# Experts 12 and 13 combined one at a time, the last expert's rows gathered during expert 14, and experts 13 and 14 added to them by padded products

## The chip, the cores and the metric

The kernel runs on one core of one Trainium2 chip. The metric is the device time in microseconds (us), the median of several runs. TensorE (PE in the views, with PEld for its weight loads), VectorE (DVE), ScalarE (ACT), GpSimd (POOL) and SyncE (SP) each work through a queue of their own in order, and wait for one another by semaphores. SP's queue issues the DMA transfers of the weights.

## The reference

One layer on 512 tokens of 1024 numbers: three attention branches, a gated sum, a norm, and then a mixture of 16 experts, in which every expert chooses its 64 best tokens, followed by a second norm. The change lies in the experts and the second norm alone:

```python
    gate, idx = lax.top_k(jnp.swapaxes(aff, 1, 2), cap)      # cap = 64 tokens for each of 16 experts
    xs = x[bidx, idx]
    h = jnp.einsum('becd,edf->becf', xs, w_gate_up)
    hg, hu = jnp.split(h, 2, axis=-1)
    ye = jnp.einsum('becf,efd->becd', jax.nn.silu(hg) * hu, w_down)
    ye = ye * gate[..., None].astype(ye.dtype)
    return jnp.zeros_like(x).at[bidx, idx].add(ye)
...
        x = layer_norm(DN_ALPHA * x + ffn, ln2_g[l], ln2_b[l])
```

## The kernel before

**An expert.** Expert e has 12 MB of float32 weights, which come from memory in blocks of 2 MB, and of 1 MB at the end. `gate_up(e, (k,))` multiplies the 64 chosen rows by slice k of the first weights (k = 0 to 7, eight matmul instructions for each k, shown as `g` x4 and `u` x4, line 1328). `act_h` makes the hidden rows on ACT and DVE, `h_transpose` turns them on PE (`ht`, line 1370, with a copy to `hT` on ACT), and `down(e)` multiplies them by the second weights (`y`, 32 instructions, line 1384). `down` then splits its result into a high and a low part by `hi_lo`, once for each half of the columns: a cast on ACT (line 103), then a subtraction on DVE (line 104).

**The order of the work** is written out by hand in the loop over e, and each engine keeps it. For the middle experts: `gate_up` for k below `lead(e)` (4, and 2 for expert 14, 1 for expert 15), just ahead of the last of these the function `full_mode(e)`, then `down(e - 1)`, then `gate_up` for the other k. So expert e - 1 is finished inside expert e.

**The combine.** The 64 result rows of an expert are added to their tokens' rows in `acc` (4 blocks m of 128 tokens, each of two halves o of 512 columns) by a product with a 0/1 matrix. `slots_T(pr)` makes that matrix on PE (`gT`, line 1407) and ACT copies it to SBUF as `GT` or `GTe`. Experts are combined in pairs: `combine(pr, half)` adds pair pr to two blocks m, with two products (high and low part) into a PSUM bank `cb` for each m and o (8 products in all, line 1468), and a DVE addition to `acc` behind each bank (line 1476). Banks of the tag `mm` are three, used in turn. Pair 5 (experts 10 and 11) is combined in the `full_mode` of experts 13 and 14, pair 6 (12 and 13) in expert 14 behind k = 3 and k = 5, and expert 14 alone in expert 15 by `combine_last`, whose products use two banks `ab`, with the norm's sums taken on the way.

**The last expert's rows** take a shorter way: the 64 rows of expert 15 are gathered from `acc` into the bank `zb` by `last_rows` (line 1551: blocks 0 and 1 at the start of expert 15, blocks 2 and 3 at its end, when expert 14 is already in these). Since blocks 0 and 1 are gathered before expert 14 is added, `last_own` adds expert 14's share to them by two products with `same` (a matrix of slots that hold the same token, made by `same_rows` and padded with zeros to write both halves). `last_down` then adds the products of the second weights straight onto `zb` (line 1577), and norms these rows and scatters them over the output. The other tokens are normed and written to the output by `norm_mean` to `norm_bias` while expert 15 runs (ACT lines 1528 and 1542, POOL line 1545).

**SP's queue** issues the weight blocks in order. Each issue waits until its place in SBUF is free, and until the block eight places earlier has landed.

Of the kernel before, what the change touches and what calls it, by code (L numbers as in the profile page):

```python
# [9 lines left out]
F32 = mybir.dt.float32  # L10
# [34 lines left out]
def pair_of(e):  # L45
    return divmod(e, 2)

# [28 lines left out]
def layer_kernel(ctx: ExitStack, tc: tile.TileContext, xt, xn, first0, wu, bgate, rpb, gains, wrt,  # L76
# [935 lines left out]
    run(g_na_proj())  # L1012
    top = cp.tile([48, 64], F32, name="top")

# [361 lines left out]
    def down(e):  # L1376
        hT = HT.pop(e)
        y = PB("Y", f"y{e}")
        for k in range(4):
            w = ring.get("dn", e, k)  # L1380
            for j in range(2):
                hf, c = divmod(2 * k + j, 4)
                for o in range(2):
                    nc.tensor.matmul(y[o * 64:o * 64 + 64], hT[:, c, hf * 64:hf * 64 + 64],  # L1384
                                     w[j][:, o * 512:(o + 1) * 512],
                                     start=(k == 0 and j == 0), stop=(k == 3 and j == 1))
            ring.done("dn", e, k)
        pr, ep = pair_of(e)
        if ep == 0:
            both = R("VS" if pr % 2 else "raw", [P, 2, D], f"y{pr}", F32R)  # L1390
            YP[pr] = (both[:, 0], both[:, 1])
        yh, yl = YP[pr]
        r = slice(ep * 64, ep * 64 + 64)
        for o in range(2):
            c = slice(o * 512, (o + 1) * 512)
            if pr == 7:
                hi_lo(yh[:64, c], yh[64:, c], y[o * 64:o * 64 + 64])
            else:
                hi_lo(yh[r, c], yl[r, c], y[o * 64:o * 64 + 64])

    GT = {}

    def slots_T(pr):
        qd, h = divmod(pr, 2)
        gp = PB("mm", f"gT{pr}", (P, NT, P))
        for m in range(NT):
            nc.tensor.matmul(gp[:, m], OH[qd][:, m, h * P:(h + 1) * P], id16, start=True, stop=True)
        if pr < 2:
            homes.append(R("tmp", [P, NT, P], "GT", F32R, bufs=2) if pr else R("bf", [P, NT, P], "GTe", F32R))
        GT[pr] = g = homes[1 + pr % 2]  # L1410
        if pr < 7:
            nc.scalar.copy(g, gp)
        else:
            for i in (0, 64):
                nc.scalar.copy(g[i:i + 64], gp[:64])

# [54 lines left out]
    def combine(pr, half):  # L1471
        for m in (2 * half, 2 * half + 1):
            for o in range(2):
                cb = PB("mm", f"cb{pr}{m}{o}")
                a = add_part(cb, pr, m, o, YP[pr])
                nc.vector.tensor_tensor(a, a, cb, op=ALU.add)  # L1476

    def combine_last(m, sums, banks):
        for o in range(2):
            a = add_part(banks[o], 7, m, o, YP[7][:1])  # L1480
            nc.vector.scalar_tensor_tensor(a, banks[o], 1.0, a, op0=ALU.mult, op1=ALU.add, accum_out=sums[:, m, o:o + 1])
# [65 lines left out]

    def last_rows(zb, ms):
        for m in ms:
            for o in range(2):  # L1550
                nc.tensor.matmul(zb[o * 64:o * 64 + 64], LATE["oh"][:, m], acc_of(m)[:, o * 512:o * 512 + 512],
                                 start=(m == 0), stop=False)

    def same_rows(sm):
        oh = OH[3]
        for m in range(2):
            nc.tensor.matmul(sm[:, :CAP], oh[:, m, 2 * CAP:], oh[:, m, last], start=(m == 0), stop=(m == 1))
        t = R(ring.free_at_end.pop(0), [P, 3, CAP], "same", F32R)
        nc.gpsimd.memset(t[:, 0:3:2].bitcast(F32), 0.0)
        for i in (0, 64):  # L1560
            nc.scalar.copy(t[i:i + 64, 1], sm[:64, :CAP])
        t = t.rearrange("p a s -> p (a s)")
        LATE["same"] = [t[:, CAP:], t[:, :2 * CAP]]

    def last_own(zb):
        y = YP[7][0]
        for o in range(2):
            nc.tensor.matmul(zb, LATE["same"][o], y[:, o * 512:o * 512 + 512], start=False, stop=False)

# [30 lines left out]
    def full_mode(e):  # L1600
# [7 lines left out]
        elif e == 4:  # L1608
            residual_rows(0)
        elif e == 5:  # L1610
            combine(0, 1)
        elif e > 5:
            combine((e - 3) // 2, (e + 1) % 2)
        if e % 2 and e > 3 or e == NEXP - 2:
            slots_T(e // 2)
        if e < 3 or e == NEXP - 2:
            h_transpose(e - 1)

    for e in range(NEXP):
        if e == 0:  # L1620
# [3 lines left out]
            all_of(g0)  # L1624
        elif e < NEXP - 1:
            for k in range(lead(e)):
                if k == lead(e) - 1:
# [17 lines left out]
            for k in range(lead(e), KD):  # L1645
                if e == 2 and k == lead(e):
                    steps(nrm)
                gate_up(e, (k,))
                if e == 1 and k == 5:
# [5 lines left out]
                elif e == 12 and k == 5:  # L1655
                    late_row(0)
                    late_row(1)
                elif e == 13 and k == 5:
                    late_half(2, "gh")
                    late_half(3, "bh")  # L1660
                    slot_tables()
                elif e == NEXP - 2 and k in (3, 5):
                    combine(6, k // 5)
        else:
            gate_up(e, (0,))
            zb, *ab = (PB("mm", f"end{i}") for i in range(3))
            last_rows(zb, (0, 1))
            h_transpose(e - 1, ab[0])
            down(e - 1)
            for m in range(NT):  # L1670
                gate_up(e, (1 + m,))
                if m == 0:
                    same_rows(ab[1])
                    LATE["g"] = [ln_row(2, h, f"g2{h}", "ST"[h]) for h in range(2)]
# [15 lines left out]
            last_own(zb)  # L1690
            last_rows(zb, (2, 3))
            last_down(zb, last_transpose(h, (ab[0], PB("Y", "htl"))))
# [131 lines left out]
```

## Time and profile before

| what | us |
|---|---|
| median of 3 runs | 949.57 (948.92 to 949.93) |
| the profiled execution, its own time | 948.83 |
| its span | 947.1 |
| PE busy | 923.2 (97%) |
| DVE, ACT, POOL busy | 432.7, 281.9, 104.2 |

The span is the profiler's stretch from the first to the last instruction, and the time holds 1.7 us around it. All points in time below are us from the span's start. A PE row's duration ends at a modelled end that lies after the next row's start, so what a piece of PE work costs is read as the distance between the starts of two rows.

### The profile page before, as it was taken

The page shows a single profiled execution, that of the slowest core. Times are in us where ns is not written, and L with a number is a line of the kernel's source. Part 1 is how long each engine was busy: PE and PEld are TensorE (multiplying, and loading weights), DVE is VectorE, ACT ScalarE, POOL GpSimd, SP SyncE. Part 2 cuts the span into 40 slices and gives each one's busy share as a digit, 9 for nine tenths or more (in the row PEclk, how much of TensorE's full clock was granted, in tenths as well). Part 3 has the DMA queues.
Part 4 walks back from the last instruction along what each step waited for, and adds up shares of the span by engine and source line. Part 5 has one row for each costly group of instructions (what it writes and reads, how often), then busy time and mean ns, then how long its engine had stood idle before and what let it go on. Part 6 is the DMA issues. An engine that isn't in the chain of part 4 may idle for free.

```text
span 947.1 us, 12783 instructions
## 1 busy us (share of the span) xinstructions
PE 923.2 (97%) x5200; PEld 599.7 (63%) x5200; DVE 432.7 (46%) x795; ACT 281.9 (30%) x532; POOL 104.2 (11%) x123
## 2 busy tenths in 40 slices
PE   9999999999999999999999999999999998999996
PEld 8899888788888888888886433533353333533334
DVE  6347659775476576237454111562232222322233
ACT  5434443654444454233242111110010100111122
POOL 0102303000122231000023004000000000000005
PEclk9999999999999999999999999999999999999999
DMA  9322221221433322566929999999999999999996
GB/s 362 120 68 67 68 67 45 67 76 37 117 98 100 104 84 69 228 246 255 381 75 381 422 427 421 421 427 427 428 428 428 426 430 425 428 428 428 427 421 260
DMA packets 40282, 251.41 MB, mean 265 GB/s; under 512 B 13136, under 2 KB 13520, under 8 KB 24992
## 3 DMA queue, kind: packets, MB, share of 16 engines
q1 hardware_dynamic: 40144, 250.34, 66.1%
q8 instruction: 41, 0.67, 0.3%
q0 software_dynamic: 80, 0.26, 0.1%
q14 instruction: 17, 0.14, 0.0%
HBM read 247.44 MB, written 2.36 MB: 264 GB/s over the span
## 4 chain that ended last, share of the span: by engine, by line
PE 79%; DMA 12%; DVE 5%; ACT 2%; issue 1%; POOLq 0%; POOL 0%; ACTq 0%; SPq 0%; DVEq 0%
DMA w<-in_wx 12%; PE g L1328 9%; PE u L1328 9%; PE y L1384 8%; PE gate L286 4%; PE gate L288 4%; PE gate L287 4%; PE cb L1468 2%; PE pr L286 2%; PE pr L287 2%; PE pr L288 2%; PE nqk L287 2%; PE nqk L288 2%; PE nqk L286 2%; PE ga L1288 1%; PE pv L662 1%
## 5 line engine op out<-in xcount | busy, mean ns | idle before, releaser
L1328 PE MATMUL g<-w,xs 128*64 128x512 f32 x508 | 132.7, 601 | 9.7 <-DMA w<-in_wx 9.6
L1328 PE MATMUL u<-w,xs 128*64 128x512 f32 x508 | 130.6, 592 | 0.0
L1384 PE MATMUL y<-w,hT 128*64 128x512 f32 x480 | 105.6, 592 | 0.7 <-ACT hT L1374 0.7
L104 DVE TENSOR_TENSOR y<-y,y 64x512 fp32r<-64x512 f32 x30 | 20.7, 689 | 146.2 <-ACT y L103 146.2
L1328 PEld LDWEIGHTS u<-w,xs 128*64 128x64 f32 x508 | 36.5, 137 | 72.5 <-issue 72.2
L1328 PEld LDWEIGHTS g<-w,xs 128*64 128x64 f32 x508 | 32.6, 136 | 72.6 <-issue 52.6
L104 DVE TENSOR_TENSOR los<-raw_twin,whi 128x1024 fp32r<-128x1024 f32 x41 | 53.6, 1307 | 53.5 <-ACT whi L103 53.5
L1384 PEld LDWEIGHTS y<-w,hT 128*64 128x64 f32 x480 | 34.3, 137 | 69.0 <-issue 65.4
L288 PE MATMUL gate<-xh,los 128*128 128x512 f32 x192 | 74.8, 390 | 0.0
L1476 DVE TENSOR_TENSOR acc<-acc,cb 128x512 f32<-128x512 f32 x56 | 34.7, 681 | 56.9 <-PE cb L1468 56.9
L103 ACT CAST y<-y 64x512 fp32r<-64x512 f32 x30 | 17.4, 580 | 139.9 <-PE y L1384 128.7
L286 PE MATMUL gate<-xh,whi 128*128 128x512 f32 x144 | 57.0, 396 | 0.0
L287 PE MATMUL gate<-xl,whi 128*128 128x512 f32 x144 | 56.1, 389 | 0.0
L103 ACT CAST whi<-raw_twin 128x1024 fp32r<-128x1024 f32 x41 | 43.0, 1049 | 9.2 <-PE wo L1126 6.5
L288 PEld LDWEIGHTS gate<-xh,los 128*128 128x128 f32 x192 | 36.0, 188 | 7.6
L104 DVE TENSOR_TENSOR los<-raw_twin,los 128x1024 fp32r<-128x1024 f32 x20 | 25.2, 1262 | 19.0 <-ACT los L103 19.0
L639 ACT ACTIVATE att_twin<-gs,nm 128x512 f32<-128x512 f32 x32 | 21.7, 684 | 39.3 <-DVE nm L638 39.3
L1374 ACT COPY hT<-ht 128x512 f32<-128x512 f32 x14 | 8.2, 586 | 78.3 <-PE ht L1370 78.3
L1339 DVE SCALAR_TENSOR_TENSOR tg<-tg,g 128x512 f32<-128x512 f32 x15 | 10.3, 687 | 45.8 <-ACT tg L1338 45.8
L286 PEld LDWEIGHTS gate<-xh,whi 128*128 128x128 f32 x144 | 27.1, 188 | 5.6 <-issue 0.2
L287 PEld LDWEIGHTS gate<-xl,whi 128*128 128x128 f32 x144 | 27.1, 188 | 5.3
L1338 ACT ACTIVATE tg<-g 128x512 f32<-128x512 f32 x15 | 9.0, 597 | 71.5 <-PE g L1328 66.5
(431 smaller groups left out, 1823.3 us busy)
## 6 DMA issues: line engine op xcount, KB each, us to landing
w<-in_wx SPq DMA_DIRECT2D x74, 2048.0 KB
w<-in_wx SPq DMA_DIRECT2D x43, 1024.0 KB
raw_twin<-in_wu SPq DMA_DIRECT2D x65, 512.0 KB
raw<-in_wu SPq DMA_DIRECT2D x8, 512.0 KB
xr<-in_xt SPq DMA_DIRECT2D x4, 512.0 KB
macc<-in_xn SPq DMA_DIRECT2D x2, 1024.0 KB
out<-xo SPq DMA_DIRECT2D x4, 512.0 KB
first<-in_first SPq DMA_DIRECT2D x4, 384.0 KB
```

Source lines behind the costliest of these rows:

```text
L103: nc.scalar.copy(hi, src)
L104: nc.vector.tensor_tensor(lo, src, hi.bitcast(F32), op=ALU.subtract)
L286: nc.tensor.matmul(acc, w_h, rh[:, k], start=(k == 0), stop=False)
L287: nc.tensor.matmul(acc, w_h, rl[:, k], start=False, stop=False)
L288: nc.tensor.matmul(acc, w_l, rh[:, k], start=False, stop=(k == nk - 1))
L639: nc.scalar.activation(self.p[:, h], self.s[h], AF.Exp, bias=nm[:, h:h + 1], accum_out=self.sm[:, h:h + 1])
L662: nc.tensor.matmul(y[h * 64:h * 64 + 64, j * P:j * P + P], ST["vg"][:, kc, kvh * 64:kvh * 64 + 64], self.pt[:, h, kc], start=(kc == 0), st ...
L1328: nc.tensor.matmul(GU[e][b][hf * 64:hf * 64 + 64], xs, w[b][hf] if isinstance(w[b], list) else w[b][:, hf * 512:hf * 512 + 512], start=(k ...
L1339: nc.vector.scalar_tensor_tensor(th, th, 1.0, g, op0=ALU.add, op1=ALU.mult)
L1384: nc.tensor.matmul(y[o * 64:o * 64 + 64], hT[:, c, hf * 64:hf * 64 + 64], w[j][:, o * 512:(o + 1) * 512], start=(k == 0 and j == 0), stop= ...
L1468: nc.tensor.matmul(cb, GT[pr][:, m], part[:, c], start=(n == 0), stop=(n == len(parts) - 1))
L1476: nc.vector.tensor_tensor(a, a, cb, op=ALU.add)
```

## The change

Expert 12 and expert 13 no longer form a pair: pairs 6, 7 and 8 are now experts 12, 13 and 14, one each, whose high part lies in rows 0 to 63 and whose low part in rows 64 to 127, so that one product does for both. `combine(5, 1)` moves from expert 14 to expert 13, behind k = 4. `combine_one(6)` adds expert 12 in expert 13 in steps of one product and one addition: two steps ahead of k = 5, three ahead of k = 6, three ahead of k = 7. `combine_one(7)` adds expert 13 in expert 14, two steps ahead of each of k = 3 to 6. `slots_T(6)` now makes the matrices of experts 12 and 13 in expert 13, with four copies on ACT, and `slots_T(8)` that of expert 14. `last_rows` gathers all four blocks in the `full_mode` of expert 14, when experts 0 to 12 are in `acc`, and `same_rows` and `last_own` bring in both expert 13 and expert 14: four products each instead of two. The three banks `zb` and `ab` are taken at the start of expert 14. The tile `same` and its zeros are made once, early, and `top` lies in a tile that exists already.

```diff
 def pair_of(e):
-    return divmod(e, 2)
+    return (e - 6, 0) if e >= 12 else divmod(e, 2)
...
-    top = cp.tile([48, 64], F32, name="top")
+    top = rt[:48, 7]
...
-            if pr == 7:
+            if pr >= 6:
                 hi_lo(yh[:64, c], yh[64:, c], y[o * 64:o * 64 + 64])
...
-    def slots_T(pr):
-        qd, h = divmod(pr, 2)
-        gp = PB("mm", f"gT{pr}", (P, NT, P))
+    def slots_T(pr, bank=None):
+        qd, h = divmod(min(pr, 7), 2)
+        gp = PB("mm", f"gT{pr}", (P, NT, P)) if bank is None else bank.rearrange("p (m b) -> p m b", m=NT)
...
-        GT[pr] = g = homes[1 + pr % 2]
-        if pr < 7:
-            nc.scalar.copy(g, gp)
-        else:
+        if pr < 6:
+            GT[pr] = homes[1 + pr % 2]
+            nc.scalar.copy(GT[pr], gp)
+            return
+        for j in range(2 if pr == 6 else 1):
+            GT[pr + j] = g = homes[1 + (pr + j) % 2]
             for i in (0, 64):
-                nc.scalar.copy(g[i:i + 64], gp[:64])
+                nc.scalar.copy(g[i:i + 64], gp[64 * j:64 * j + 64])
...
+    def combine_one(pr, banks=None):
+        for i in range(2 * NT):
+            m, o = divmod(i, 2)
+            cb = banks[o] if banks else PB("mm", f"cb{pr}{m}{o}")
+            a = add_part(cb, pr, m, o, YP[pr][:1])
+            nc.vector.tensor_tensor(a, a, cb, op=ALU.add)
+            yield
...
-    def last_rows(zb, ms):
-        for m in ms:
+    def last_rows(zb):
+        for m in range(NT):
...
     def same_rows(sm):
         oh = OH[3]
-        for m in range(2):
-            nc.tensor.matmul(sm[:, :CAP], oh[:, m, 2 * CAP:], oh[:, m, last], start=(m == 0), stop=(m == 1))
...
+        for m in range(NT):
+            nc.tensor.matmul(sm[:, :CAP], oh[:, m, CAP:3 * CAP], oh[:, m, last], start=(m == 0), stop=(m == NT - 1))
+        for j in range(2):
+            for i in (0, 64):
+                nc.scalar.copy(same_t[i:i + 64, 1 + 2 * j], sm[64 * j:64 * j + 64, :CAP])
...
     def last_own(zb):
-        y = YP[7][0]
-        for o in range(2):
-            nc.tensor.matmul(zb, LATE["same"][o], y[:, o * 512:o * 512 + 512], start=False, stop=False)
+        t = same_t.rearrange("p a s -> p (a s)")
+        for j in range(2):
+            y = YP[7 + j][0]
+            for o in range(2):
+                c = (2 * j + 1 - o) * CAP
+                nc.tensor.matmul(zb, t[:, c:c + P], y[:, o * 512:o * 512 + 512], start=False, stop=False)
...
-        elif e > 5:
+        elif 5 < e < NEXP - 2:
             combine((e - 3) // 2, (e + 1) % 2)
-        if e % 2 and e > 3 or e == NEXP - 2:
+        if e % 2 and 3 < e < 13:
             slots_T(e // 2)
-        if e < 3 or e == NEXP - 2:
+        if e < 3:
             h_transpose(e - 1)
+        elif e == NEXP - 2:
+            slots_T(8, ab[1])
+            h_transpose(e - 1, ab[0])
+            last_rows(zb)
...
+                elif e == 13 and k > 4:
+                    for _ in range((2, 3, 3)[k - 5]):
+                        steps(c12)
+                elif e == NEXP - 2 and 2 < k < 7:
+                    steps(c13, c13)
                 gate_up(e, (k,))
...
+                elif e == 13 and k == 4:
+                    combine(5, 1)
+                    slots_T(6)
+                    c12 = combine_one(6)
...
-                elif e == NEXP - 2 and k in (3, 5):
-                    combine(6, k // 5)
+                elif e == NEXP - 2 and k == 2:
+                    same_rows(ab[1])
+                    c13 = combine_one(7, ab)
...
-            last_rows(zb, (0, 1))
             h_transpose(e - 1, ab[0])
...
             last_own(zb)
-            last_rows(zb, (2, 3))
             last_down(zb, last_transpose(h, (ab[0], PB("Y", "htl"))))
```

Three places of PE's queue show what moves. The first is expert 13 from k = 4 on; before, its slices of the first weights (`w_3806`, `w_3866`) follow one another, with only the rows of the norm (`gh`, `bh`) and of the scatter (`ix`) between them:

```order
L1328 MATMUL g_6038<-w_3806,xs_5843 64x512 x2
L1328 MATMUL u_6039<-w_3806,xs_5843 64x512 x2
...
L1497 MATMUL gh<-gb,gsel 64x512 x2
L1497 MATMUL bh<-gb,gsel 64x512 x2
...
L1516 MATMUL ix<-rows_id,oh_5814 64x2
L1328 MATMUL g_6038<-w_3866,xs_5843 64x512 x2
L1328 MATMUL u_6039<-w_3866,xs_5843 64x512 x2
```

In the changed kernel the same stretch (the slices are `w_3805` and `w_3865` here) holds pair 5's second half, the new matrices and the steps of expert 12:

```order
L1328 MATMUL u_6040<-w_3805,xs_5844 64x512 x2
L1470 MATMUL cb_6109<-y_5810,GT 128x512 x2
...
L1407 MATMUL gT_6125<-tri_d,oh_5815 128x128
L1470 MATMUL cb_6134<-y_6100,GTe 128x512
L1470 MATMUL cb_6137<-y_6100,GTe 128x512
L1328 MATMUL g_6039<-w_3805,xs_5844 64x512 x2
...
L1470 MATMUL cb_6165<-y_6100,GTe 128x512
L1470 MATMUL cb_6168<-y_6100,GTe 128x512
L1470 MATMUL cb_6171<-y_6100,GTe 128x512
L1328 MATMUL g_6039<-w_3865,xs_5844 64x512 x2
L1328 MATMUL u_6040<-w_3865,xs_5844 64x512 x2
```

What moved in is `combine(5, 1)` (`y_5810`) and `slots_T(6)`, and right behind them the first products that read the new `GTe`. The second place is expert 14 from the end of k = 0 to k = 4; before:

```order
L1328 MATMUL u_6154<-w_3936,xs_5842 64x512 x2
L1468 MATMUL cb_6160<-y_5809,GT 128x512 x2
...
L1370 MATMUL ht_6183<-ident,h_6149 128x128 x4
L1328 MATMUL g_6153<-w_3936,xs_5842 64x512 x2
...
L1384 MATMUL y_6194<-w_4292,hT 64x512 x8
L1328 MATMUL g_6153<-w_3398,xs_5842 64x512 x2
...
L1468 MATMUL cb_6229<-y_6105,GTe 128x512 x2
L1468 MATMUL cb_6233<-y_6105,GTe 128x512 x2
...
L1328 MATMUL g_6153<-w_3462,xs_5843 64x512 x2
```

And now, where `end_6197` is `zb`, `end_6198` and `end_6199` are the banks `ab`, and `y_6252` is expert 13's result:

```order
L1328 MATMUL u_6201<-w_3935,xs_5843 64x512 x2
...
L1370 MATMUL end_6198<-ident,h_6193 128x128 x4
L1561 MATMUL end_6197<-acc,late 64x512 x8
L1328 MATMUL g_6200<-w_3935,xs_5843 64x512 x2
...
L1384 MATMUL y_6231<-w_4291,hT 64x512 x8
L1328 MATMUL g_6200<-w_3398,xs_5843 64x512 x2
...
L1570 MATMUL end_6199<-oh_5815 128x64
L1470 MATMUL end_6198<-y_6252,GT 128x512
L1470 MATMUL end_6199<-y_6252,GT 128x512
L1328 MATMUL g_6200<-w_3398,xs_5843 64x512 x2
```

The gathering (line 1561) has come in where a combine stood, and the steps of expert 13 now follow one slice after its `down`, where the pair's combine stood two slices after it. The third place is the end of expert 15, ahead of the last products; before, and then now:

```order
L1328 MATMUL u_6285<-w_4292,xs_5843 64x512 x2
L1568 MATMUL end_6290<-y_6319,same 128x512 x2
L1551 MATMUL end_6290<-acc,late 64x512 x4
L1362 MATMUL end_6291<-ident,h_6413 128x128 x2
L1362 MATMUL htl<-ident,h_6413 128x128 x2
L1577 MATMUL end_6290<-w_3398,hTl 64x128 x32
```

```order
L1328 MATMUL u_6315<-w_4291,xs_5843 64x512 x2
L1581 MATMUL end_6197<-y_6252,same 128x512 x2
L1581 MATMUL end_6197<-y_6342,same 128x512 x2
L1362 MATMUL end_6198<-ident,h_6430 128x128 x2
L1362 MATMUL htl<-ident,h_6430 128x128 x2
L1590 MATMUL end_6197<-w_3398,hTl 64x128 x32
```

The gathering of blocks 2 and 3 is gone from here, and expert 13's two padded products have come in.

## Rows read from the trace of the kernel before

**Rows 1.** The page: the span.

```profile
span 947.1 us, 12783 instructions
```

**Rows 2.** The chain that ended last, 780 to 947.1: start, duration, what.

```profile
846.70 39.08 DMA w<-in_wx
...
885.82 1.08 PE g L1328 x4
```

**Rows 3.** Waits of PE from 861.3 on: total, times, longest.

```profile
PE g L1328 <- DMA w<-in_wx: 2.5, 3, 1.2
```

**Rows 4.** Windows: length, busy time of PE, PEld, DVE, ACT, POOL, granted clock, DMA share, GB/s.

```profile
861.36:885.82 24.46, 22.99 (x112) 8.03 (x113) 5.10 (x11) 4.67 (x8) 0.00 (x0) 1.00 1.01 427
885.82:932.38 46.56, 45.59 (x198) 16.18 (x198) 21.23 (x42) 13.54 (x23) 10.96 (x16) 1.00 1.01 422
```

**Rows 5.** Timeline of PE, expert 13's k = 4 to expert 14's k = 2: start, duration.

```profile
861.36 1.08 PE L1328 MATMUL g<-w,xs 128*64 128x512 f32 x4 [1.21 <-DMA w<-in_wx]
...
869.56 1.03 PE L1328 MATMUL u<-w,xs 128*64 128x512 f32 x4
871.14 1.08 PE L1328 MATMUL g<-w,xs 128*64 128x512 f32 x4 [0.54 <-DMA w<-in_wx]
...
873.01 2.25 PE L1468 MATMUL cb<-y,GT 128*128 128x512 f32 x8
875.12 0.38 PE L1407 MATMUL gT<-tri_d,oh 128*128 128x128 f16 x4
875.73 0.66 PE L1370 MATMUL ht<-ident,h 128*128 128x128 f32 x4 [0.22 <-DVE acc L1476]
...
878.08 7.04 PE L1384 MATMUL y<-w,hT 128*64 128x512 f32 x32
885.82 1.08 PE L1328 MATMUL g<-w,xs 128*64 128x512 f32 x4 [0.70 <-DMA w<-in_wx]
```

**Rows 6.** Timeline of PE, expert 14's k = 3 to expert 15's k = 1.

```profile
889.40 2.25 PE L1468 MATMUL cb<-y,GTe 128*128 128x512 f32 x8
891.58 1.08 PE L1328 MATMUL g<-w,xs 128*64 128x512 f32 x4
...
902.55 1.89 PE L1551 MATMUL end<-acc,late 128*64 128x512 f32 x8
...
905.75 7.09 PE L1384 MATMUL y<-w,hT 128*64 128x512 f32 x32 [0.73 <-ACT hT L1374]
912.67 1.03 PE L1328 MATMUL g<-w,xs 128*64 128x512 f32 x4
```

**Rows 7.** Timeline of PE, expert 15's k = 2 to 7.

```profile
916.06 1.08 PE L1328 MATMUL g<-w,xs 128*64 128x512 f32 x4
...
918.59 1.08 PE L1328 MATMUL g<-w,xs 128*64 128x512 f32 x4
...
925.42 1.03 PE L1328 MATMUL g<-w,xs 128*64 128x512 f32 x4
...
927.14 1.03 PE L1328 MATMUL g<-w,xs 128*64 128x512 f32 x4
```

**Rows 8.** Timeline of ACT and DVE, 875 to 888.

```profile
875.54 1.17 ACT L1415 CAST GT<-gT 64x512 fp32r<-64x512 f32 x2 [5.17 <-PE gT L1407]
...
887.11 0.69 DVE L104 TENSOR_TENSOR y<-y,y 64x512 fp32r<-64x512 f32 x1 [0.65 <-ACT y L103]
```

**Rows 9.** Timeline of all engines, 928 to 933: the end of expert 15.

```profile
928.96 0.73 PE L1568 MATMUL end<-y,same 128*128 128x512 f32 x2
...
930.39 1.15 ACT L1542 ACTIVATE xo<-xo,l2y 128x1024 f32<-128x1024 f32 x1 [1.35 <-POOL l2y L1533]
930.44 0.48 DVE L1352 SCALAR_TENSOR_TENSOR h<-tg,gw,u 128x256 f32<-128x256 f32 x1
...
931.96 0.37 ACT L1363 COPY hTl<-end 128x256 f32<-128x256 f32 x1 [0.42 <-PE end L1362]
...
932.38 7.21 PE L1577 MATMUL end<-w,hTl 128*64 128x128 f32 x128 [0.24 <-ACT hTl L1363]
```

More of the change, by code (lines that the diff above doesn't have):

```diff
@@ L1476, in combine @@
                 nc.vector.tensor_tensor(a, a, cb, op=ALU.add)
+    def combine_one(pr, banks=None):
[5 more added lines that the diff above has]
+            yield
     def combine_last(m, sums, banks):
         for o in range(2):
-            a = add_part(banks[o], 7, m, o, YP[7][:1])
+            a = add_part(banks[o], 8, m, o, YP[8][:1])
             nc.vector.scalar_tensor_tensor(a, banks[o], 1.0, a, op0=ALU.mult, op1=ALU.add, accum_out=sums[:, m, o:o + 1])
@@ L1552, in last_rows @@
                                  start=(m == 0), stop=False)
+    same_t = small([P, 5, CAP], "same", F32R, bufs=1)
+    nc.gpsimd.memset(same_t[:, ::2].bitcast(F32), 0.0)
     def same_rows(sm):
         oh = OH[3]
-        for m in range(2):
-            nc.tensor.matmul(sm[:, :CAP], oh[:, m, 2 * CAP:], oh[:, m, last], start=(m == 0), stop=(m == 1))
[L1558 to L1563, printed above, removed]
-    def last_own(zb):
-        y = YP[7][0]
-        for o in range(2):
-            nc.tensor.matmul(zb, LATE["same"][o], y[:, o * 512:o * 512 + 512], start=False, stop=False)
+        for m in range(NT):
[3 more added lines that the diff above has]
+                nc.scalar.copy(same_t[i:i + 64, 1 + 2 * j], sm[64 * j:64 * j + 64, :CAP])
+    def last_own(zb):
+        t = same_t.rearrange("p a s -> p (a s)")
[4 more added lines that the diff above has]
+                nc.tensor.matmul(zb, t[:, c:c + P], y[:, o * 512:o * 512 + 512], start=False, stop=False)
     def last_down(zb, hT):
@@ L1625, in layer_kernel @@
         elif e < NEXP - 1:
+            if e == NEXP - 2:
+                zb, *ab = (PB("mm", f"end{i}") for i in range(3))
             for k in range(lead(e)):
@@ L1661, in layer_kernel @@
                     slot_tables()
-                elif e == NEXP - 2 and k in (3, 5):
-                    combine(6, k // 5)
+                elif e == NEXP - 2 and k == 2:
+                    same_rows(ab[1])
+                    c13 = combine_one(7, ab)
         else:
             gate_up(e, (0,))
-            zb, *ab = (PB("mm", f"end{i}") for i in range(3))
-            last_rows(zb, (0, 1))
             h_transpose(e - 1, ab[0])
@@ L1672, in layer_kernel @@
                 if m == 0:
-                    same_rows(ab[1])
                     LATE["g"] = [ln_row(2, h, f"g2{h}", "ST"[h]) for h in range(2)]
```

## Prediction

> **What bounds the kernel now.** I read the end of the program first, because the change touches nothing ahead of expert 13 except two small tiles. The chain of waits shows the turn [rows 2]: up to 885.8 us it runs through weight transfers, one after another for 39 us at a time, and from there through PE alone to the end. So from 885.82 on whatever PE sheds is gained, unless something else comes last. That invites the thought that work taken away behind 885.82 and put ahead of it is free. How much room is there ahead of it? PE's own waits from 861.3 on answer this: three waits for weights, 2.5 us in all, and the longest of them, 1.2, is the first [rows 3]. The timeline says where they lie: at 861.36 (expert 13's k = 4), at 871.14 (expert 14's k = 0) and at 885.82 (its k = 2) [rows 5]. The windows say that in the whole stretch from 861.36 to 932.38 DMA is full (share 1.01, 427 and 422 GB/s), that PE is busy for all but 2.4 us, and that its clock is granted in full, 2.4 GHz [rows 4]. DMA and PE therefore run neck and neck here, and DMA is ahead from 885.82 on. The reader is to see that the last wait for weights that lies ahead of all moved work is the one at 861.36: it ends when a block lands, which the change doesn't touch. From that point I walk along PE's queue, before and after, to the start of the last products at 932.38 [rows 9], and what lies behind these is the same in both kernels.
>
> **A. Expert 13, from 861.36 to expert 14's first slice.** Five things come in.
> Pair 5's second half costs what it costs now in expert 14: 2.1 us (873.01 to 875.12) [rows 5].
> Behind it stands `slots_T(6)`, and right behind that the first product that reads `GTe`. The nearest row is expert 14's own matrix: its PE work starts at 875.12 [rows 5], and ACT's two casts end at 875.54 + 1.17 = 876.71 [rows 8]. That is 1.6 us, in which PE has 0.25 us of its own to do and then stands, since its queue keeps order: k = 5, `gh`, `bh` and `ix` are all behind. With the signal's way to PE I take 1.65. The lower bound is 1.1 (the first cast alone), the upper 2.8 (PE waits for all four casts, 1.17 more). Before, the same work of `slots_T(6)` stood ahead of 861.36 and hid in that wait.
> Then the eight products of expert 12. A slice alone takes 1.72 (925.42 to 927.14) and a slice with a pair of such products 2.53 (916.06 to 918.59) [rows 7], so a pair costs 0.81. A chain of eight takes 2.18 between the starts around it [rows 6], some 2.3 with the same slower slices at its sides, so each product beyond the pair costs (2.3 - 0.8)/6 = 0.25, and a group of three 1.05. The first pair follows a stall and a combine whose edges are counted there: 0.7. Two groups of three: 2.1. Edges of the combine: 0.1. The group ahead of k = 6 takes its banks from `gh`, `bh` and `ix`, which ACT and DVE must first have copied: nothing to 0.6, I take 0.2, since those copies run while `ix` is worked on.
> What falls away is the wait for weights at 871.14. The view puts it at 0.54 behind a modelled end; by starts it is 871.14 - 869.56 - 0.86 (half a slice) = 0.72 [rows 5]. Sum: 2.1 + 1.65 + 0.7 + 2.1 + 0.1 + 0.2 - 0.7 = **+6.1**. The DVE additions of these products (0.6 to 0.7 each) run beside PE and end before the gathering needs them.
>
> **B. Expert 14 up to k = 2.** Pair 5's half leaves (-2.1), and with it the 0.2 that `ht` waited for its addition. The gathering of four blocks comes in: 1.89 for two of them by its row, less the overlap at the edge [rows 6], so 3.5 to 3.6 for four. The wait at 885.82 falls away: `y` takes 6.92 (905.75 to 912.67) [rows 6], it took 7.74 here (878.08 to 885.82) [rows 5], so -0.8. Sum: **+0.4**. Expert 14's k = 2 starts 6.5 late, at 892.3.
>
> **C. Expert 14's k = 2 to expert 15's `down(14)`.** The two chains of eight leave: -4.6. The four pairs of expert 13 come: +3.25. `same_rows` with four small products costs 0.3 here, and half as much leaves expert 15. A new wait: the first pair now stands one slice behind `down(13)`. The second half of expert 13's result is split 887.11 + 0.69 - 878.08 = 9.72 after the first product of `y` [rows 5, 8]. PE gets to the pair's second product 6.9 + 1.8 + 0.3 + 0.3 = 9.3 after it, and its bank must also be read out by four small casts of `same` that stand behind `y`'s casts on ACT. Nothing to 1.1; I take 0.7. The gathering of two blocks leaves expert 15's start: -1.85. `h_transpose(14)` still waits 0.73 for its copy. Sum: -4.6 + 3.25 + 0.15 + 0.7 - 1.85 = **-2.35**.
>
> **D. The end of expert 15.** From the last slice PE now has four products of `last_own` instead of two, and no gathering: 0.5 more, 1.9 less. But look at what stands there on ACT: the norm's scaling of block 3 runs from 930.39 to 931.54, and the copy of `hTl`, for which the last products wait, is behind it in ACT's queue. It runs at 931.96 now, 0.42 after ACT became free [rows 9]. With PE early it runs at 931.55, and no earlier: **-0.4**. If that scaling were not in the way, the second half of `h` at 930.92 would bound it, and 1.0 would be gained.
>
> **The rest costs nothing.** The early zeros of `same` are one small POOL instruction among its many, and `top` moves between tiles that DVE uses in the same order. The block issues on SP that wait for expert 13's and 14's slices come up to 6 us later, but seven blocks of 2 MB at 427 GB/s [rows 4], an estimate of 34 us of transfers, are in flight then, so DMA does not run dry, and PE, being later at each block than now, waits for none. The outputs follow PE's delay and still land ahead of the scatter.
>
> **The sum.** 6.1 + 0.4 - 2.35 - 0.4 = +3.75, of which I take 3.6, since the edges that I counted twice weigh some tenths. On the profiled execution (span 947.1 [rows 1], time 948.83) that gives 952.4; on the median of the runs shown, 949.57, which lies 0.7 higher, 953.2. I forecast **952.8**.
>
> **The rivals.**
> *The room ahead is enough (faster).* If PE reached k = 2 of expert 14 at 885.82 as it does now, only C and D would count: -2.35 - 0.4 = -2.75, so about 946.5. It decides at 6.5 us of waits between 861.36 and 885.82; rows 3 and 5 show 0.7 + 0.2 + 0.8 = 1.7. What speaks for it is the chain, which gives that stretch to DMA. 0.08.
> *The small waits don't come (no change).* If the matrix copies, the banks and expert 13's split are all hidden (-1.4, -0.2, -0.7) by work that I read at another place than it has, +1.3 is left: 950.5. Nothing in PE's queue stands between `gT` and its first reader, which speaks against it. 0.10.
> *The groups cost only their streams (no change).* In a long run one product of 512 columns takes 6.92 / 32 = 0.216 [rows 6]. If the sixteen products in seven groups took that alone, 3.5 instead of the 6.05 in A and C, +1.0 would be left: 950.2. The pair's 0.81 [rows 7] speaks against it, for two streams are 0.43 of that. 0.04.
> The Trainium skill's page TensorE: Matmul & The Clock Gate (Part 2, Step-by-step) has the rule behind this rival: PE pulls weight loads ahead of matmuls that are in flight, while the matmuls keep their order, so that splitting a chain would cost nothing; by its 216 ns for a matmul of 512 columns the sixteen would take 3.45. By that rule the sum is +1.0, by the trace's pair it is +3.6, and the trace does not agree with the rule at the edge between a slice of the weights and a combine.
> *PE waits for all four matrix copies.* 1.17 more [rows 8], +4.8: 954.0. 0.14.
> *As summed*, +2 to +4.3: 0.64.
>
> **How the numbers follow.** A measurement of this kernel can tell about 0.2%, 1.9 us, from no change. Above +1.9 lie the sum and the case of four copies, 0.78; within it the two of no change, 0.14; below it the first, 0.08. The range from +1.3 (950.6) to +5.2 (954.5) leaves out the faster case and most of the two of no change; the ends are those of the wait for `GTe` (1.1 and 2.8) and of expert 13's split (0 and 1.1) around the sum.
>
> **What the profile would show.** Right: no wait of PE for weights behind 861.4; a wait for ACT of some 1.3 us at the first product of expert 12; expert 14's k = 2 starting near 892; a wait of some 0.7 between the two products of the first pair in expert 14; `hTl` copied directly behind the scaling of block 3; the last products starting near 936. Wrong: if PE still waits for weights at expert 14's k = 2, there was room that I didn't see, and the first rival has it; if the groups of two and three cost under 0.6, the rule on weight loads holds; if the chain at the end runs through the outputs, I have misjudged POOL's or SP's part.

## The result, and the profile after

The changed kernel takes 954.58 us in the median of 5 runs (952.74 to 955.07), the kernel before 949.30 beside it; the ratio is 1.0051, with a 95% interval of 1.0036 to 1.0066. It is slower by 5.3, where the prediction had summed 3.6: the forecast was 952.8, from 950.6 to 954.5, and this median lies 0.1 above that range's upper end. Five more runs of the same kernel (below, `e5_again`) gave 953.67. The profiled execution took 954.75, its span is 953.0.

The timeline of PE in the changed kernel, from expert 13's k = 4 to the last products, answers to [rows 5], [rows 6] and [rows 9]: start, duration, line, what, and in brackets what PE waited for.

```profile
862.30 1.08 PE L1328 MATMUL g<-w,xs 128*64 128x512 f32 x4 [1.24 <-DMA w<-in_wx]
...
867.93 0.73 PE L1470 MATMUL cb<-y,GTe 128*128 128x512 f32 x2 [1.27 <-ACT GTe L1417]
868.59 1.08 PE L1328 MATMUL g<-w,xs 128*64 128x512 f32 x4
...
870.46 1.07 PE L1507 MATMUL gh<-gb,gsel 8*64 8x512 f32 x4
...
872.32 0.30 PE L1526 MATMUL ix<-rows_id,oh 128*64 128x2 f16 x8
872.55 1.79 PE L1470 MATMUL cb<-y,GTe 128*128 128x512 f32 x3
874.27 1.98 PE L1328 MATMUL g<-w,xs 128*64 128x512 f32 x4
876.03 1.18 PE L1328 MATMUL u<-w,xs 128*64 128x512 f32 x4
877.14 0.97 PE L1470 MATMUL cb<-y,GTe 128*128 128x512 f32 x3
878.04 1.08 PE L1328 MATMUL g<-w,xs 128*64 128x512 f32 x4
...
879.80 1.03 PE L1328 MATMUL g<-w,xs 128*64 128x512 f32 x4
...
894.46 1.03 PE L1328 MATMUL g<-w,xs 128*64 128x512 f32 x4
...
897.53 0.50 PE L1470 MATMUL end<-y,GT 128*128 128x512 f32 x1 [0.65 <-ACT same L1573]
...
912.23 7.09 PE L1384 MATMUL y<-w,hT 128*64 128x512 f32 x32 [0.72 <-ACT hT L1374]
...
935.38 1.20 PE L1581 MATMUL end<-y,same 128*128 128x512 f32 x4
...
938.28 3.93 PE L1590 MATMUL end<-w,hTl 128*64 128x128 f32 x68 [0.29 <-ACT hTl L1363]
```

Behind 861.4 PE waits for weights once, at 862.30; the waits at expert 14's k = 0 and k = 2 are gone. The distance between the same landmarks before [rows 5, 6, 9] and after gives each term:

| stretch | before | after | change | forecast |
|---|---|---|---|---|
| A: expert 13's k = 4 to expert 14's k = 0 | 9.78 | 17.50 | +7.72 | +6.1 |
| B: to expert 14's k = 2 | 14.68 | 14.66 | -0.02 | +0.4 |
| C: to `down(14)` | 19.93 | 17.77 | -2.16 | -2.35 |
| expert 15's slices (905.75 to 928.96 before) | 23.21 | 23.15 | -0.06 | 0 |
| D: to the last products | 3.42 | 2.90 | -0.52 | -0.4 |

They make +4.96. The rest of the 5.90 by which the last products start later, 0.94, lies ahead of 862.30 and is of this one execution: the second profile of the same kernel has its k = 4 at 861.36, the very time of before.

Inside A the two groups of three products `cb` stand out, which should take the same. The first lasts until 874.27, 1.72 between starts, the second 0.90 (877.14 to 878.04). The slice behind the first takes 1.76 for `g` alone, where others take 0.86 to 0.91. A window of the same kernel says why (length, busy PE, PEld, DVE, ACT, POOL, granted clock, DMA share, GB/s):

```profile
872.90:876.30 3.40, 3.30 (x9) 1.27 (x10) 2.07 (x4) 0.13 (x1) 0.00 (x0) 0.50 0.99 424
```

The granted clock is 0.50 there, 1.2 GHz of 2.4, in a stretch in which the view has PE busy for 3.3 of 3.4 us. Before, it was 1.00 throughout [rows 4]. The price is read against a profile of the same order in which the clock stays (`e1_gt_early`, below): from `ix` to expert 14's k = 0 it takes 872.24 to 878.23, 5.99; here 872.32 to 879.80, 7.48. So 1.5 of A is the clock's, and A without it is +6.2. Not all of the first group's 1.72 is the clock's: at full clock, in `e1_gt_early`, this group takes 1.23 (872.47 to 873.70), 0.33 more than the second, because its second product waits until ACT has copied `bh` out of a bank (there the copy ends at 872.36 + 0.59, and the weights of that product are loaded at 873.04).

At the end, the chain that ended last (start, duration, what) shows the last step of D, as forecast: `hTl` is copied when the scaling of block 3 on ACT ends.

```profile
929.99 2.38 POOL xo L1555
...
933.53 2.35 POOL xo L1555
...
936.82 1.15 ACT xo L1552
937.97 0.27 ACT hTl L1363
```

It shows one thing more. The scaling waits for `l2y` on POOL, and this stands in POOL's queue behind the additions for the output, `xo`, of 2.4 us each. So from 925.5 to the copy the chain lies on DVE, POOL and ACT, where before it ran through PE and `hTl` was copied 0.42 after ACT became free [rows 9]. Ahead of 925.5 the view gives the chain to DMA, although PE waits for no weights behind 862.30.

### The profile page after: what moved, and what is told of

Its sections match the earlier page's. It is cut to its first block, busy times and chain, and to the rows that moved or that the text cites. A ratio compares the mean times of both kernels' runs of the same rounds, so it can differ in the third digit from the quotient of the medians.

```text
span 953.0 us, 12799 instructions
## 1 busy us (share of the span) xinstructions
PE 927.4 (97%) x5204; PEld 600.3 (63%) x5204; DVE 438.1 (46%) x803; ACT 284.0 (30%) x537; POOL 104.5 (11%) x123
## 4 chain that ended last, share of the span: by engine, by line
PE 73%; DMA 15%; DVE 6%; ACT 2%; POOL 2%; issue 1%; POOLq 0%; SPq 0%; ACTq 0%; DVEq 0%
DMA w<-in_wx 14%; PE g L1328 8%; PE u L1328 7%; PE y L1384 6%; PE gate L286 4%; PE gate L288 4%; PE gate L287 4%; PE pr L286 2%; PE pr L287 2%; PE pr L288 2%; PE cb L1470 2%; PE ga L1288 2%; PE nqk L288 2%; PE nqk L286 2%; PE nqk L287 2%; PE ga L1290 1%
## 5 line engine op out<-in xcount | busy, mean ns | idle before, releaser
L1478 DVE TENSOR_TENSOR acc<-acc,cb 128x512 f32<-128x512 f32 x48 | 29.7, 682 | 50.9 <-PE cb L1470 50.9
```

## The experiments

The theory was: PE has only some 1.7 us of waits ahead of 885.8, so that moved work costs in full, and the clock falls because PE stands still at `GTe`. The rivals: there is room; the fall has another cause. Kernels with the same time of before in the table ran on one chip, beside it. The mean granted clock of a run counts the falls: with none it is 0.998 or 0.999 (the end of the program behind the last products runs at half clock), and 3.4 us at half clock take 0.002 from it. It does not tell where a fall lies. A run at 0.997 may also have none, since the half clock at the end lasts 2.6 us in the profile of before and 4.6 in that of `e11_packed2`, which is 0.001 of the mean.

| kernel | median (runs) | before | ratio, 95% | runs at 0.997 or less |
|---|---|---|---|---|
| changed | 954.58 (5) | 949.30 | 1.0036 to 1.0066 | 4 of 5 |
| e1_gt_early | 952.79 (6) | 949.38 | 1.0024 to 1.0048 | 5 of 6 |
| e2_fill | 954.38 (5) | 949.38 | 1.0043 to 1.0071 | 3 of 5 |
| e3_room | 960.20 (4) | 949.38 | 1.0102 to 1.0133 | 1 of 4 |
| e4_packed | 948.46 (11) | 949.38 | 0.9981 to 0.9999 | 5 of 11 |
| e5_again | 953.67 (5) | 949.25 | 1.0030 to 1.0057 | 4 of 5 |
| e6_fill6 | 954.36 (5) | 949.25 | 1.0031 to 1.0058 | 4 of 5 |
| e7_apart | 953.01 (5) | 949.25 | 1.0026 to 1.0053 | 0 of 5 |
| e8_stall | 956.23 (5) | 949.25 | 1.0060 to 1.0087 | 5 of 5 |
| e9_triple_away | 953.41 (5) | 949.24 | 1.0030 to 1.0057 | 2 of 5 |
| e10_both | 952.58 (6) | 949.24 | 1.0021 to 1.0045 | 0 of 6 |
| e11_packed2 | 948.15 (11) | 949.24 | 0.9980 to 0.9998 | 5 of 11 |

### Is there room ahead of 885.8?

`e3_room`, on the kernel before (`fill(56)` makes 56 products of `ident` with itself in a bank that nobody reads):

```diff
+                elif e == 13 and k == 4:
+                    fill(56)
```

> The kernel before, with 56 additional products of the identity with itself (128x128, some 0.11 us each, 6.2 us together) into a bank that nobody reads, behind expert 13's k = 4, where the change puts its work; nothing else is changed and nothing waits. My theory (of PE's room ahead of 885.8 there are 1.7 us in waits for weights): 6.2 - 1.7 = 4.5 come through to the end, about 953.8, and the wait for weights at expert 14's k = 2 is gone. Rival (the chain gives this stretch to DMA, so there is room for about 6 us): at most 0.5 more than the kernel before, 949.8, and the wait at k = 2 gets shorter by all that was added. Rival (DMA gives way too, since its blocks wait for PE to release their places): 6 us or more, 955.5.

The size was wrong: each of these products is two instructions, and PE took 12.7 us for them. The timeline of PE in this kernel:

```profile
860.93 1.08 PE L1328 MATMUL g<-w,xs 128*64 128x512 f32 x4 [1.20 <-DMA w<-in_wx]
...
862.79 12.77 PE L1603 MATMUL fill<-ident 128*128 128x128 f32 x112
...
943.09 7.21 PE L1577 MATMUL end<-w,hTl 128*64 128x128 f32 x128 [0.24 <-ACT hTl L1363]
```

and its windows, the first over these products:

```profile
862.80:875.50 12.70, 12.70 (x115) 12.58 (x113) 0.00 (x0) 0.00 (x0) 0.00 (x0) 1.00 1.01 428
875.50:890.00 14.50, 14.29 (x75) 5.55 (x76) 4.22 (x8) 3.51 (x6) 0.00 (x0) 1.00 1.00 426
```

12.7 went in. By the medians 10.8 came out at the end (960.20 - 949.38), so 1.9 was absorbed; by the starts in this profile, from k = 4 to the last products, it is 82.16 against 71.02 before [rows 5, 9], so 1.6 was absorbed. The theory had 1.7, the first rival 6, and the second none. DMA ran on at 426 to 428 GB/s while PE fell ten microseconds behind. So there was little room, and being late at the blocks did not slow the transfers up to 890. With 12.7 instead of 6.2 the forecasts are 11.0, 6.7 and 12.7.

### The wait for the matrix

`e1_gt_early` (the first two lines stand in `full_mode`; `js=(0,)` copies expert 12's matrix alone, `js=(1,)` expert 13's):

```diff
+        elif e == 13:
+            slots_T(6, js=(0,))
...
                     combine(5, 1)
-                    slots_T(6)
+                    slots_T(6, js=(1,))
```

> The changed kernel, with expert 12's matrix made at the start of expert 13 and only expert 13's behind the combine of pair 5, so that no product has to wait for a matrix just made. My theory (PE has next to no room between 861 and 886, and the granted clock fell to 0.50 from 872.9 to 876.3 because PE stood still for 1.27 us at that matrix shortly before): the wait of about 1.3 is gone, the clock stays at 1.00, which gives another 1.6, and 0.2 to 0.3 for the separate matrix comes back: about 2.7 us less than the changed kernel, near 951.8, and still 2 to 3 above the kernel before. Rival (the fall of the clock has nothing to do with that wait): the clock falls in expert 13 all the same and only about 1.0 is gained, near 953.5. Rival (PE has room in that stretch, the delay comes from elsewhere): what PE sheds here turns into waits for weights, 954 to 955.

`e8_stall` goes the other way:

```diff
-        for j in range(2 if pr == 6 else 1):
+        for j in ((1, 0) if pr == 6 else (0,)):
```

> The changed kernel with the copies in the other order: expert 13's matrix is copied first, expert 12's behind it, so that PE's wait at expert 12's first product grows by two casts of 0.58 each, from 1.27 to 2.4. Theory (PE has no room here, and the fall belongs to this wait): 1.2 more than the changed kernel, and every run at 0.996 or below, near 955.9. Rival (the fall has another cause): 1.2 more run by run, with as many runs at 0.998 as the changed kernel has. Rival (room ahead of 885.8): the time of the changed kernel.

The timeline of PE in `e1_gt_early`:

```profile
862.86 1.08 PE L1328 MATMUL g<-w,xs 128*64 128x512 f32 x4 [1.20 <-DMA w<-in_wx]
...
867.52 1.06 PE L1470 MATMUL cb<-y,GTe 128*128 128x512 f32 x2 [0.31 <-DVE acc L1478]
...
872.24 0.30 PE L1526 MATMUL ix<-rows_id,oh 128*64 128x2 f16 x8
872.47 1.30 PE L1470 MATMUL cb<-y,GTe 128*128 128x512 f32 x3
873.70 1.08 PE L1328 MATMUL g<-w,xs 128*64 128x512 f32 x4
...
878.23 1.03 PE L1328 MATMUL g<-w,xs 128*64 128x512 f32 x4
```

and in `e8_stall`:

```profile
869.10 0.74 PE L1470 MATMUL cb<-y,GTe 128*128 128x512 f32 x2 [2.45 <-ACT GTe L1417]
```

In the first the wait of 1.27 is replaced by one of 0.31 for the addition that frees a bank, and the pair takes 0.33 longer; term A is 15.37, or 0.64 less than the 16.0 that it has without the fall. In the second the wait is 2.45, 1.18 more, and A is 1.30 longer (18.80). The medians lie 1.2 below and 2.2 above 954.0, the median of the changed kernel's eight runs at 0.996 (below); in the second, three of five runs have 0.993 or 0.994, more than one fall. So the wait costs about its length, less what comes in its place, and the long one may bring a second fall. All five runs of the second are at 0.996 or below, as the theory had it, but that can't be told from eight of ten; and five of six runs of the first are still at 0.997 or less. In its profile the fall lies elsewhere, at 790, directly behind the longest wait for weights, ahead of the stretch that the change touches. A window of it, and the end of that wait, first in this kernel and then in the changed one:

```profile
790.00:793.00 3.00, 3.00 (x10) 0.79 (x7) 0.00 (x0) 0.00 (x0) 0.00 (x0) 0.50 1.00 426
```

```profile
789.45 1.48 PE L1328 MATMUL g<-w,xs 128*64 128x512 f32 x4 [2.67 <-DMA w<-in_wx]
```

```profile
788.91 1.08 PE L1328 MATMUL g<-w,xs 128*64 128x512 f32 x4 [2.79 <-DMA w<-in_wx]
```

Such a wait does not bring a fall each time: in the changed kernel it took 2.79 and in `e6_fill6` 2.78, and in both the clock stayed at 1.00 behind it.

### Does the wait bring the fall of the clock?

`e2_fill`, and `e6_fill6` with 6 in the place of 12:

```diff
                     slots_T(6)
+                    fill(12)
                     c12 = combine_one(6)
```

> The changed kernel, with twelve additional products of the identity with itself (128x128, some 0.11 us each) into a bank that nobody reads, placed where PE stands for expert 12's matrix: PE works through the wait, and the wait for the matrix ends at the same time. My theory (the clock falls because PE stood still): the granted clock stays at 1.00 through expert 13, and about 1.6 us are gained although nothing is shortened, near 953.0. Rival (the clock falls for another reason): the clock falls as before and the time is that of the changed kernel or 0.2 above, 954.6.

> The additional products in the right number: six of the identity with itself, each of which turned out to be two instructions of 0.114 us, 1.37 us together, just as long as PE stands for expert 12's matrix. Theory (the fall of the clock belongs to that wait): hardly a run at 0.996, and near 952.8 though no work is less. Rival (the fall has another cause): as many runs at 0.996 as the changed kernel has, and its time, near 954.5.

> The changed kernel once more, unaltered, for a second profile and more runs. Of its runs so far, those with a mean granted clock of 0.996 took 953.4 to 955.1 and the one with 0.998 took 952.7; the profiled one had a stretch of 3.4 us at half clock, 1.7 of 953 us, which is that difference. Theory (the fall belongs to this kernel's stretch from 866 on, where PE stands for 1.27 us at the matrix): most runs again at 0.996, and the profile again with half clock between 868 and 880. Rival (a fall comes now and then anywhere behind a wait, and only costs time where PE sets the pace): the profile has it elsewhere, behind a wait for weights, or not at all. Both: runs at 0.996 near 954.5, those at 0.998 near 952.8.

In `e2_fill` the twelve took 2.66 us, twice the wait, so PE was 1.2 later behind it; its profile has no fall, but three of its five runs are at 0.996. It decides nothing. `e6_fill6` does. The timeline of PE there:

```profile
866.14 1.56 PE L1616 MATMUL fill<-ident 128*128 128x128 f32 x12
867.57 0.74 PE L1470 MATMUL cb<-y,GTe 128*128 128x512 f32 x2
...
872.20 1.79 PE L1470 MATMUL cb<-y,GTe 128*128 128x512 f32 x3
```

and its windows:

```profile
866.10:872.50 6.40, 6.40 (x43) 3.05 (x40) 2.41 (x6) 3.33 (x6) 0.00 (x0) 1.00 1.01 428
872.54:875.95 3.41, 3.33 (x9) 1.27 (x10) 2.08 (x4) 0.13 (x1) 0.00 (x0) 0.50 0.99 423
```

PE works through the wait for the matrix, and the fall comes all the same, at the same place of its queue. `e5_again` has it there too:

```profile
861.36 1.08 PE L1328 MATMUL g<-w,xs 128*64 128x512 f32 x4 [1.24 <-DMA w<-in_wx]
...
871.39 0.30 PE L1526 MATMUL ix<-rows_id,oh 128*64 128x2 f16 x8
871.62 1.79 PE L1470 MATMUL cb<-y,GTe 128*128 128x512 f32 x3
```

```profile
871.90:875.20 3.30, 3.25 (x9) 1.13 (x10) 2.13 (x5) 0.20 (x1) 0.00 (x0) 0.51 0.98 417
```

My theory of the wait for the matrix fell here. In all four profiles with a fall in expert 13 (changed, `e5_again`, `e6_fill6`, `e8_stall`) it comes directly behind `gh`, `bh` and `ix`, in the three products of expert 12, where the second of them waits some 0.3 us for the bank of `bh`. `e1_gt_early` and `e2_fill` have the same order and the same 0.3, and no fall there in their profiles, so the order does not bring it every time. The next two kernels take these products apart.

`e7_apart`:

```diff
                 elif e == 13 and k == 5:
                     late_half(2, "gh")
+                elif e == 13 and k == 6:
                     late_half(3, "bh")
                     slot_tables()
```

> The changed kernel with the rows of the norm taken apart: gh stays behind k = 5, bh and ix go behind k = 6, so that these products of 8 rows no longer follow one another. PE's work is the same. Theory (the fall belongs to the wait for the matrix at 866.6): no change, near 954.5, most runs at 0.996. Rival (the profiled fall began at 872.9, directly behind gh, bh and ix, and these small products bring it): hardly a run at 0.996, near 952.8.

`e9_triple_away`:

```diff
-                    for _ in range((2, 3, 3)[k - 5]):
+                    for _ in range((2, 0, 3)[k - 5]):
...
+                elif e == 13 and k == 7:
+                    all_of(c12)
```

> The changed kernel with gh, bh and ix in a row as it has them, and with expert 12's three products that stand directly behind ix moved behind k = 7. PE's work is the same. Theory (the clock falls behind gh, bh and ix by themselves, 2.1 us of products of 8 rows and 2 columns): most runs at 0.996 as before, the profile with half clock directly behind ix, near 954. Rival (the three products belong to it, for the kernel before has gh, bh and ix in a row too, with a slice of the weights behind them, and rarely falls): hardly a run at 0.996, near 952.9.

The timeline of PE and two windows of `e7_apart`, and then the window of `e9_triple_away` behind `ix`:

```profile
862.78 1.08 PE L1328 MATMUL g<-w,xs 128*64 128x512 f32 x4 [1.25 <-DMA w<-in_wx]
...
868.41 0.73 PE L1470 MATMUL cb<-y,GTe 128*128 128x512 f32 x2 [1.27 <-ACT GTe L1417]
...
879.24 1.03 PE L1328 MATMUL g<-w,xs 128*64 128x512 f32 x4
```

```profile
872.00:875.00 3.00, 2.98 (x14) 0.91 (x12) 1.88 (x3) 0.59 (x1) 0.00 (x0) 1.00 1.03 431
875.00:878.00 3.00, 2.90 (x21) 1.13 (x21) 1.54 (x5) 0.59 (x1) 0.00 (x0) 1.00 1.00 426
```

```profile
871.70:875.00 3.30, 3.30 (x23) 1.24 (x22) 1.21 (x4) 0.56 (x1) 0.00 (x0) 1.00 0.99 417
```

With `gh` and `bh` apart the wait of 1.27 is unchanged and no run of five shows a fall, with `e10_both` (below) none of eleven, where the order of the change has eight of ten. The 0.3 for the bank of `bh` is still there (the weights of the first two products are loaded at 876.23 and 876.80), so it is not enough by itself. The gain in A is the 1.5 less 0.45, by which the two rows and the products behind them now take longer: 862.78 to 879.24 is 16.46. With the three products moved away, `gh`, `bh` and `ix` in a row are not enough for a fall in the profile, as they were not before the change; two runs of five show 0.997, which leaves open whether the clock fell in these. That kernel doesn't get its gain in full, since the products behind k = 7 delay the hidden rows on DVE, and PE waits for these:

```profile
880.18 0.66 PE L1370 MATMUL end<-ident,h 128*128 128x128 f32 x4 [0.70 <-DVE h L1340]
```

`e10_both` has the edits of `e1_gt_early` and `e7_apart` together.

> The changed kernel with two repairs at once: expert 12's matrix early, as in e1_gt_early, and gh and bh apart, as in e7_apart. Theory (a wait of 1.27 and a fall of the clock worth 1.5 are two terms of their own, and the rest of the delay is PE's work, which has no room): the clock at 0.998 in every run, 1.0 below e7_apart, near 952, still 2 to 3 above the kernel before. Rival (the two are one): the time of e1_gt_early or e7_apart, 952.8 to 953.

Its timeline:

```profile
861.96 1.08 PE L1328 MATMUL g<-w,xs 128*64 128x512 f32 x4 [1.20 <-DMA w<-in_wx]
...
866.62 1.07 PE L1470 MATMUL cb<-y,GTe 128*128 128x512 f32 x2 [0.31 <-DVE acc L1478]
...
877.78 1.03 PE L1328 MATMUL g<-w,xs 128*64 128x512 f32 x4
```

Its A is 861.96 to 877.78, 15.82, and its median lies 3.3 above the kernel before: 0.4 below `e7_apart`, not 1.0, since the wait at `GTe` comes back in part as the wait for a bank and the slower pair, 0.64. What is left when the fall and most of the wait are gone is PE's moved work.

### The same work in other places

`e4_packed` (its main lines, on the changed kernel; the first stands in `full_mode`, with `slots_T(6)` behind it, the fourth group behind `down(12)`, and the last lines ahead of `norm_scale(3)`; the lines that these replace, in expert 13 behind k = 4 and 5 and in expert 14 behind k = 2, are taken out):

```diff
+        elif e == 13:
+            combine(5, 1)
...
-            last_rows(zb)
+            last_rows(zb, (0, 1, 2))
+            same_rows(ab[1])
...
+                elif k == 1 and e == 13:
+                    late_half(2, "gh")
...
+            elif e == 13:
+                late_half(3, "bh")
+                slot_tables()
...
-                elif e == NEXP - 2 and 2 < k < 7:
+                elif e == NEXP - 2 and k > 3:
                     steps(c13, c13)
...
+                elif e == 11 and k == 5:
+                    combine(4, 1)
...
+                elif e == 12 and k == 6:
+                    combine(5, 0)
...
+            last_own(zb)
+            last_rows(zb, (3,))
+            hTl = last_transpose(h, (ab[0], PB("Y", "htl")))
```

> The changed kernel with the same work laid where PE waited for weights in the kernel before, and with no product right behind the matrix that it needs: the second half of pair 4 in expert 11, the halves of pair 5 in experts 12 and 13 ahead of their full slices, expert 12's and 13's matrices at the start of expert 13, the rows of the norm and the scatter one slice apart, expert 13's products one slice later in expert 14, blocks 0 to 2 of the last expert's rows gathered in expert 14 and block 3 at the end, and the copy of the last hidden rows ahead of the norm's scaling of block 3 on ACT. My theory (what counts is only where PE's work lies against its waits for weights, up to 885.8, and the waits that PE's queue makes for itself): the clock stays up, the work moved ahead of 861 is hidden in waits there, the end waits 0.9 less; in all 946 to 949, below the kernel before. Rival (the waits ahead of 861 are needed by DMA all the same, since each later slice releases its place later): 951 to 953.

`e11_packed2`, on top of it, moves the line that makes `LATE["g"]` from expert 15's first slice to between `h_transpose(14)` and `down(14)`.

> The kernel of e4_packed with the two products of the norm's rows for expert 15 moved from behind its k = 1 to ahead of expert 14's second weights, where PE stands 0.72 us for the copy of hT. In e4_packed PE waits 1.09 for the last quarter of these weights afterwards. Theory (behind that wait PE sets the pace, and 0.66 of its work leaves): 0.5 to 0.7 less than e4_packed, near 947.9. Rival (the end is set by the last weights on DMA): the time of e4_packed, 948.5.

The timeline of PE in `e4_packed`:

```profile
910.54 1.94 PE L1384 MATMUL y<-w,hT 128*64 128x512 f32 x8 [1.09 <-DMA w<-in_wx]
...
931.58 7.21 PE L1590 MATMUL end<-w,hTl 128*64 128x128 f32 x128 [0.24 <-ACT hTl L1363]
```

and in `e11_packed2`:

```profile
910.64 1.94 PE L1384 MATMUL y<-w,hT 128*64 128x512 f32 x8 [1.11 <-DMA w<-in_wx]
...
915.32 0.51 PE L1470 MATMUL end<-y,GTe 128*128 128x512 f32 x1 [0.59 <-DVE y L104]
```

The packed order beats both kernels: 0.9 below the one before, by an interval that just leaves out no change, and 5 to 6 below the change. Several pieces moved at once, and the runs do not tell what each of them brings. PE now waits for weights again, at 910.54, so that ahead of it there is room where the change had none. What remains behind that wait is PE's work to 931.58, 0.8 earlier than before [rows 9]. Taking 0.66 more out of it, in `e11_packed2`, gave a new wait of 0.59 at once: the first pair of expert 14 came too early for the split of its result. Its 0.3 is less than these runs can tell apart.

## Why the prediction came out as it did

**The bound** was read rightly. `e3_room` shows 1.6 to 1.9 us of room where rows 3 and 5 gave 1.7, and the rival of room enough is out. No wait of PE for weights is left behind 862.30, as announced.

**Term A** is where the miss lies: +7.72 for +6.1. The wait at `GTe` was 1.27, for an announced 1.3, and it ended with the first two casts, so the rival of all four copies is out; `e8_stall` made that rival, at 1.2 more. Three products at full clock took 0.90 between starts, and the slices at such groups' sides 1.76 (878.04 to 879.80) and 1.87 (868.59 to 870.46, with `gh` behind it) instead of 1.72 [rows 7], which together is the estimate of 1.05. The wait for the banks of `gh` and `bh`, put at 0.2, is 0.33 in `e1_gt_early`. What failed is the step that took TensorE's clock as granted in full, as rows 4 had it. The change put three products behind `gh`, `bh` and `ix`; in both profiles of the changed kernel the clock fell there to half, which cost 1.5 us, and eight of its ten runs are at 0.996. Without the fall A is +6.2. The prediction had no term for the clock and no rival with one.

**Term B** cost 0.4 less than forecast: between the combine and what follows `ht`, PE took 1.19 before (875.12 to 876.31) and 0.77 now (881.62 to 882.39), where 0.2 of gain was counted, and the rest lies in tenths. **Term C** gave 0.2 less and **term D** 0.1 more. In C the wait of 0.7 came as 0.65, but ended with the casts of `same` and not with the split of expert 13's result: the bank had to be read out first, which I had named second. In D the scaling on ACT stood in the way as said.

The terms without the fall make 6.2 - 2.2 - 0.1 - 0.5 = +3.4, for a sum of 3.6. The two of ten runs at 0.998 took 952.74 and 952.53, 3.3 and 3.5 above the 949.25 that is the median of before in three calls; the eight at 0.996 have their median at 954.0, 4.8 above. So the forecast of 952.8 fits the runs in which the clock stays, and lacks 1.2 for the others.

**The number by itself misleads.** 954.58 lies nearest to the 954.0 of the rival of four copies, and only the wait of 1.27 in the timeline rules that rival out. The upper end of the range, 954.5, stood for late copies and a late split of expert 13's result, and neither came; that the fall of the clock reaches just to that end is luck. The lower end does not follow from what the prediction says of it: with the waits at 1.1 and 0 the sum is +2.35, and +1.3 is the value of the rival of small waits.

**The signs.** Expert 14's k = 2 started at 894.46, and at 893.50 in `e5_again`, where 892 was announced, and the last products at 938.28 and 937.34, where 936 was. One sign that I had named for a wrong reading is there: the chain at the end runs through POOL's additions for the output. D keeps its size, since the scaling starts as long after `down(14)` as before (24.59 against 24.64), but that POOL's queue holds the scaling up, and with it the last products, was not in my account.

**The rival of streams alone** (+1.0) is out with the pair: the groups took what rows 7 gave them. The Trainium skill's page TensorE: Matmul & The Clock Gate (Part 2, Step-by-step) has weight loads pulled ahead of matmuls in flight, where the row groups do not conflict or a background buffer takes them; at the edge between a slice and a combine the trace does not agree: 0.90 for three products, of which three streams are 0.65, and up to 0.15 more for the slice at their side.

## What to carry over

Room for moved work is the sum of the bounding engine's own waits ahead of the point where the other takes over, and not the length of the chain that the profile gives to a transfer: 1.6 to 1.9 of 24 us here. Where work stands decides what it costs: nearly the same operations (`e4_packed` has one small product less) cost 4.5 us more (953.74, the median of the ten runs of the changed kernel, against 949.25) or 0.9 less by where they stood against waits and against the results that they read. A wait filled up brings the next one that lies close behind it, so look for that before counting the gain.

## What the runs showed of the hardware

The granted clock fell to 0.50 for 3.4 us in a stretch in which the view has PE busy for 3.33 of 3.41 us, and for 6.40 of the 6.40 us ahead of it (`e6_fill6`). What ran just before were eight instructions on 8 rows, eight of 2 columns, and the first of three products, behind which PE stands some 0.3 us for a bank. Where a slice of the weights stood between `gh` and `bh`, no run of eleven showed a fall. The Trainium skill's page TensorE: Matmul & The Clock Gate (Part 1) has the clock fall when PE idles; the fall at 790, behind a wait of 2.67, fits that, though waits of 2.79 and 2.78 at the same place brought none, and the fall of `e6_fill6` in expert 13 comes without a wait of that kind since 861.94. Why it comes there, and only in four of six profiles of this order, stays open.

Of the 41 runs of the kernel before that stood beside the experiments, 9 are at 0.997 or less: their median is 949.65, that of the others 949.25, so if these are falls, they cost far less there than 1.5. Where they lie is not known, as these runs left no trace. Not settled either is where the fall lies in the other runs without a trace: `e1_gt_early` has five of six at 0.997 or less and `e2_fill` three of five, with none in expert 13 in their profiles, and one run of `e6_fill6` at 0.996 took 952.60, as much as its run at 0.998 (952.58).
